# Queue positions of weight, joining and sample work, and ScalarE as issuer of attention stores, in a hybrid decoder step

## The chip, the cores and the metric

The kernel runs on one core of a Trainium2 chip. The core has a matrix engine (TensorE, PE in the rows; its weight loads are listed as PEld), a vector engine (VectorE, DVE), an activation engine (ScalarE, ACT), GpSimd (POOL) and SyncE (SP), which only issues transfers. Each engine takes its instructions in the order of its own queue, and an instruction that waits holds everything behind it. Transfers (DMAs) are issued from an engine's queue and then run on 16 DMA engines. The metric is the device time of one execution in microseconds (us); lower is better. Before and after are compared by the median of several executions; the trace comes from one further execution under the hardware profiler.

## What is computed

One layer of a hybrid decoder, for 2048 prompt positions and for 8 x 8 new tokens with a window buffer of 2048 positions. Cut to what matters:

```python
h = rms_norm(x, g_norm); proj = h @ w_in                 # u, va, za, q, k, vb, zb
vn = rms_norm(va per group); mixed = tril(w_s) @ vn + b_s # mixer A, chunks of 128
a = rms_norm(u * mixed) * silu(za)
for (w, r) in ((128, 1), (512, 4), (2048, 16)):          # mixer B, 8 heads x 64
    s = q @ k.T * SCALE, masked to w // r keys at stride r
    m = max(s); p = exp(s - m); den = sum(p)
    outs += p @ v / den; lses += m + log(den)
b = rms_norm(sum_i softmax(lses)_i * outs_i) * silu(zb)
h = x + concat(a, b) @ w_out
y = h + sigmoid(h @ w_ple_gate) * rms_norm(p_emb @ w_ple)
```

The new tokens take the same steps with the cached keys and values. Keys and values of the prompt and of the new tokens and the normalised `va` rows are outputs too.

## The kernel before, in words

**Phase 1, the projection.** `w_in` is cut into eight chunks, four of mixer A (384 columns) and four of mixer B (512 columns, one pair of heads), in the order A0 B0 B1 A1 B2 B3 A2 A3. For each chunk a loop runs over 16 tiles of 128 prompt rows and one tile of 64 new tokens. A tile is 24 matrix products (L473, `gemm`) into one of three PSUM banks (`psg`): values are held as a high and a low fp16 half, so three products stand for one. Then `a_evac` or `b_evac` empties the bank: copies, squares and a tanh on ScalarE (L613 to L616, L513 to L525), and as the last reader the gate product on VectorE (L617 or L526).

**Weights' steps.** While chunk n is multiplied, `wprep` prepares chunk n+1: loads (L351, SyncE), squares on ScalarE (L367), a sum over partitions by a matrix product with ones (L274), a chain of tiny VectorE steps for the scale, then the high half on ScalarE (L391) and the low half on VectorE (L392). `wprep3` does the same for `w_ple`, `w_out` and `w_ple_gate` (loads L940, squares L949, halves L964 and L965) during the last chunk and at the start of phase 2. The main loop calls one or more steps per tile with `next(nxt)`.

**Attention.** A planner (`Pump`) deals out attention in units between the projection's products. A unit is: scores on TensorE (L823), mask and maximum on VectorE (L829), exponential and high half on ScalarE (L838, L841), low half on VectorE (L842), a transposing DMA by SyncE (L763, `pT<-pc`), and the product with the values on TensorE (`stage_c`, L869 to L871, reading `pT`). After every second slot ScalarE copies the result out of PSUM (L875, `rec`) and SyncE stores it (L883, to `r1d`, `r2d` or `r3d` by stride). There are 160 units and 96 stores. Stride 16 is dealt in the last quarter of each head pair, ahead of four units of stride 4.

**Joining.** When a head pair has all three strides, `comb_load` loads them back (L891, `rl`) and `combine` weighs them, on VectorE for the most part (L901 to L926), and stores into `catd` (L928).

**Phase 2, per tile of 128 rows.** `p3_load` reads `catd` and x, `p3_cat` makes halves (L973 to L997) and transposes them by DMA (`Tc`), `p3_out` multiplies by `w_out`, `p3_h` does the same with the sum (`Th`), `p3_gate` multiplies by `w_ple_gate`, `p3_ple` by `w_ple` (all matrix products at L1008, `gemm2`).

**New tokens.** `sample` handles their attention for one head pair, cut into steps by `yield`: loads of cached keys and values, 16 multiplications on GpSimd (L1263) and 16 reductions on VectorE (L1264) per head pair, transposes and products on TensorE (L1243 to L1343). The planner deals these steps between phase 2's products.

**What sets the order.** The program is written in the order in which the planner deals, but a list scheduler then fixes each engine's queue: an instruction may stand ahead of one that was written earlier if, by the scheduler's own reckoning of time, its inputs are there first. `tc.issue_after(i)` adds a constraint of order only: what is written inside the block and goes to i's engine stands behind i in that engine's queue. Before, `behind()` uses it for `stage_c`, `a_mix` and some products of `sample`, always against the newest matrix product of the tile loop (`last_mm`).

## Time and profile before

| what | value |
|---|---|
| executions, us | 1469.55, 1474.05, 1478.37; median 1474.05 |
| profiled execution, us | 1471.11 |
| its span from first to last instruction, us | 1469.4 |
| mean granted TensorE clock | 0.954 |
| busy in the span: PE, DVE, ACT, POOL, us | 1296.9, 999.6, 821.8, 315.7 |
| chain of work that ended last, by kind | PE 44%, DMA 23%, DVE 14%, ACT 11% |

Times inside the trace count from the span's start. An engine counts as busy while an instruction of its own runs, not while it issues a transfer. A line of the timeline gives the start, the length, the engine, the source line and what was written from what; in square brackets stand the idle time of the engine just before it and what ended that. The list of waits adds such idle times up by who waited for whom.

### The profile page before, as it was taken

Reading aid. Unit: us, or ns where it says so; the run is one execution under the profiler, and the core shown is the slowest. Engines: PE = TensorE matmul, PEld = TensorE weight load, DVE = VectorE, ACT = ScalarE, POOL = GpSimd, SP = SyncE. Lnnn points to the kernel's source line nnn. Section 1 sums busy time; section 2 is a strip of 40 time slices with the busy share of each in tenths; the row PEclk is TensorE's granted clock in tenths of the full one; section 3 lists DMA queues with packets and bytes.
Section 4 is the critical chain, followed back from the end, with each engine's and each line's share of the span. In section 5 each row is a group of like instructions: output and inputs, shape, how many; then the busy total and the mean of one; then the engine's idle time right before and its main releaser. Section 6 shows DMA issues by size and latency. Waiting matters only on the chain.

```text
span 1469.4 us, 26262 instructions
## 1 busy us (share of the span) xinstructions
PE 1296.9 (88%) x8600; PEld 674.0 (46%) x8600; DVE 999.6 (68%) x3018; ACT 821.8 (56%) x2269; POOL 315.7 (21%) x279
## 2 busy tenths in 40 slices
PE   4899998998898897899788985569998998999998
PEld 2564454544564554455455653224443443444343
DVE  4675776777777698777778788885455456456364
ACT  5785778966679677687677884553222122123122
POOL 8221001102101111100120025311152143134001
PEclk9899999999999999999999998779999999999999
DMA  5954598799847989978996798976899799989542
GB/s 145 235 132 114 124 173 182 173 222 226 193 112 165 206 188 209 178 185 189 222 213 145 154 247 216 288 173 170 203 210 245 181 203 229 230 184 231 137 88 65
DMA packets 589592, 271.32 MB, mean 185 GB/s; under 512 B 323184, under 2 KB 571056, under 8 KB 589456
## 3 DMA queue, kind: packets, MB, share of 16 engines
q1 hardware_dynamic: 587472, 268.00, 80.7%
q0 software_dynamic: 1984, 1.66, 0.7%
q8 instruction: 67, 1.10, 0.3%
q14 instruction: 69, 0.57, 0.1%
HBM read 136.94 MB, written 55.08 MB: 131 GB/s over the span
## 4 chain that ended last, share of the span: by engine, by line
PE 44%; DMA 23%; DVE 14%; ACT 11%; issue 4%; SPq 3%; POOL 1%; DVEq 0%; ACTq 0%; POOLq 0%
PE psg L473 14%; PE psg L1008 11%; PE pss L1008 10%; DMA pT<-pc 6%; DMA rl<-r2d 2%; DVE sm L829 2%; ACT sm L838 2%; DMA K<-in_cache_k_dram 2%; DMA qB<-qd 2%; DMA wst<-in_w_in_dram 2%; PE pso L1343 2%; DVE pc L842 2%; PE pso L1248 2%; ACT kc L715 1%; DMA rl<-r3d 1%
## 5 line engine op out<-in xcount | busy, mean ns | idle before, releaser
L473 PE MATMUL psg<-wt,xT 128*128 128x512 f16 (+1 forms) x3072 | 640.6, 363 | 31.3 <-DVE agz L617 26.5
L473 PEld LDWEIGHTS <-xT 128*128 128x128 f16 x3072 | 301.7, 100 | 299.7 <-issue 44.3
L193 POOL TENSOR_TENSOR sm<-sm,mhalf 128x1 f32<-128x1 f32 (+5 forms) x115 | 145.6, 1271 | 790.4 <-DVE sm L532 324.6
L838 ACT ACTIVATE sm<-sm,rec 128x256 f32<-128x256 f32 (+1 forms) x384 | 151.7, 459 | 38.9 <-DVE rec L834 35.8
L829 DVE CUSTOM_DVE_ANT_0 sm<-pss,mask,psc 128x256 f32<-128x256 f32 (+1 forms) x384 | 145.1, 419 | 12.2 <-PE pss L823 8.5
L1008 PEld LDWEIGHTS <-Tc 128*128 128x128 f16 x800 | 76.8, 99 | 116.0 <-issue 28.5
L1263 POOL TENSOR_TENSOR K<-K,qB 96x512 f32<-96x512 f32 x64 | 94.1, 1475 | 161.2 <-DMA qB<-qd 62.3
L842 DVE TENSOR_TENSOR pc<-sm,pc 128x512 f16<-128x512 f32 (+1 forms) x160 | 104.2, 653 | 34.1 <-ACT pc L841 32.7
L1008 PEld LDWEIGHTS <-Th 128*128 128x128 f16 x800 | 76.7, 98 | 109.0 <-issue 15.3
L995 ACT ACTIVATE hl<-x,sm 128x1024 f16<-128x1024 f32 (+1 forms) x17 | 19.5, 1148 | 147.3 <-DVE sm L976 132.4
L869 PEld LDWEIGHTS <-pT 128*128 128x128 f16 x600 | 57.1, 98 | 96.1 <-DMA pT<-pc 90.5
L1008 PE MATMUL psg<-w,Th 128*128 128x512 f16 x400 | 95.8, 381 | 5.0 <-DMA Th<-hl 5.0
L841 ACT ACTIVATE pc<-sm 128x512 f16<-128x512 f32 (+1 forms) x160 | 96.0, 603 | 7.2 <-DMA pT<-pc 6.2
L1008 PE MATMUL psg<-w,Tc 128*128 128x512 f16 x400 | 97.0, 386 | 2.8 <-DMA Tc<-hl 2.8
L1264 DVE TENSOR_REDUCE blk<-K 96x8 f32<-96x512 f32 x64 | 43.4, 680 | 79.5 <-POOL K L1263 79.5
L1008 PE MATMUL pss<-w,Tc 128*128 128x512 f16 x400 | 96.0, 382 | 0.0
L1008 PE MATMUL pss<-w,Th 128*128 128x512 f16 x400 | 93.4, 379 | 0.0
L823 PEld LDWEIGHTS <-qk 128*128 128x128 f16 x960 | 74.2, 120 | 29.3 <-issue 5.9
L1100 POOL TENSOR_TENSOR tg<-tg,x 128x1024 f32<-128x1024 f32 (+1 forms) x16 | 37.6, 2348 | 153.9 <-DVE tg L1099 141.8
L869 PE MATMUL pso<-v,pT 128*128 128x65 f16 x248 | 32.2, 201 | 42.4 <-DMA pT<-pc 42.4
L869 PE MATMUL pso<-vt,pT 128*128 128x65 f16 x352 | 43.5, 195 | 28.9 <-DMA pT<-pc 28.8
L715 ACT ACTIVATE kc<-qk 128x512 f16<-128x512 f16 x72 | 58.9, 872 | 13.8 <-DMA qk<-qkd 8.5
(321 smaller groups left out, 2239.5 us busy)
## 6 DMA issues: line engine op xcount, KB each, us to landing
qB<-qd SPq DMA_DIRECT2D x64, 192.0 KB
K<-in_cache_k_dram SPq DMA_DIRECT2D x64, 192.0 KB
V<-in_cache_v_dram SPq DMA_DIRECT2D x64, 192.0 KB
vt<-vscr SPq DMA_DIRECT2D x32, 258.0 KB
K<-in_cache_k_dram SPq DMA_DIRECT2D x32, 256.0 KB
cat<-catd SPq DMA_DIRECT2D x16, 512.0 KB
x<-in_x_prompt_dram SPq DMA_DIRECT2D x16, 512.0 KB
V<-in_cache_v_dram SPq DMA_DIRECT2D x32, 256.0 KB
```

Of the source, the lines that this page charges most:

```text
L193: nc.gpsimd.tensor_tensor(y, src, mhalf[:p, :n], op=ALU.pow)
L473: last_mm[0] = nc.tensor.matmul(g[:, :ncol], lhsT=l, rhs=r, start=(n == 0), stop=(n == (23 if j < NT else 15)))
L715: nc.scalar.activation(t[:, h], src[:, h], AF.Copy)
L823: nc.tensor.matmul(pss[:, s, h, b * w:(b + 1) * w], lhsT=Q[:, h, qs], rhs=keys(h, k), start=(i == 0 and b == 0), stop=(i == 1 and b == n - 1))
L829: nc.vector.tensor_tensor_reduce(sm4[:, s, h], pss[:, s, h], mk, psc, -3.0e38, op0=ALU.add, op1=ALU.max, accum_out=mx[:, i:i + 1])
L838: nc.scalar.activation(sm4[:, s, h], sm4[:, s, h], AF.Exp, bias=r[:, sl + s, h, HD + 1:HD + 2])
L841: nc.scalar.activation(pc[:, :n], smv, AF.Copy)
L842: nc.vector.tensor_tensor(pc[:, n:2 * n], smv, pc[:, :n], op=ALU.subtract)
L869: nc.tensor.matmul(po[:, q, h, 0:65], lhsT=H, rhs=v[:, vs_, a:a + 65], start=(bi == 0), stop=False)
L1008: last_mm[0] = nc.tensor.matmul(gs[hf], lhsT=o[part][:, kt], rhs=w[:, kt % 2, half, :], start=(n[hf] == 0), stop=(n[hf] == (3 if m == P el ...
L1263: nc.gpsimd.tensor_tensor(K3, K3, qB, op=ALU.mult)
L1264: nc.vector.tensor_reduce(s3[:, b, :, ts_].rearrange("p h t -> p t h"), K3.rearrange("p t (h d) -> p t h d", d=HD), axis=AX.X, op=ALU.add)
```

## The change

Three things are changed.

1. `late()` is new. It puts what is written inside it behind the newest matrix product (`last_mm`), behind the newest full tile's gate on VectorE and tanh on ScalarE, and behind the newest transposing DMA on SyncE (of `pT`, or in phase 2 of a low half). In phase 2 the two marks of VectorE and ScalarE are renewed by `p3_out` and `p3_gate`. It wraps every step of `wprep` and `wprep3` that the tile loop or the planner calls, `combine`, and every step of `sample`. The first chunk's own weights and the steps left over at a chunk's end are not wrapped; neither are the loads of `comb_load`.
2. The 96 attention stores (L883 before, L898 after) and the 14 small copies of `fold` (L484 before, L494 after; the new tokens' half tiles) are issued by ScalarE instead of SyncE.
3. At the start, four of the eight loads of the first weights (L351) are issued by ScalarE.

```diff
+    last_on = {}
+
+    def late():
+
+        c = ExitStack()
+        for i in [last_mm[0]] + list(last_on.values()):
+            if i is not None:
+                c.enter_context(tc.issue_after(i.ins))
+        return c
...
-                    nc.sync.dma_start(t[:, k2, :ncol].rearrange("p (s c) -> p s c", c=P), src)
+                    (nc.scalar if fast and k2 else nc.sync).dma_start(
+                        t[:, k2, :ncol].rearrange("p (s c) -> p s c", c=P), src)
...
-        nc.sync.dma_start(c[:TS, :n], c[TS:, :n])
+        nc.scalar.dma_start(c[:TS, :n], c[TS:, :n])
...
+        tanh = nc.scalar.activation(th[:m], g[:m, 384:512], AF.Tanh, scale=sc[:m, 2:3])
+        gate = nc.vector.scalar_tensor_tensor(G["gz"][:m, q, :], th[:m], 1.0, g[:m, 384:512], op0=ALU.add, op1=ALU.mult)
+        if m == P:
+            last_on.update(dve=gate, act=tanh)
...
-                nc.sync.dma_start(o["pT"][:, :2 * o["n"] // P, :], o["pc"][:, :2 * o["n"]], transpose=True)
+                last_on["sp"] = nc.sync.dma_start(o["pT"][:, :2 * o["n"] // P, :], o["pc"][:, :2 * o["n"]], transpose=True)
...
-                combine(hp, jg, sc, *got)
+                with late():
+                    combine(hp, jg, sc, *got)
...
-            nc.sync.dma_start(dst[:, s0:s0 + 2], rc)
+            nc.scalar.dma_start(dst[:, s0:s0 + 2], rc)
...
-            yield from sample(hp)
+            steps = sample(hp)
+            while True:
+                with late():
+                    dt = next(steps, None)
+                if dt is None:
+                    break
+                yield dt
...
                 for _ in range(1 if ci else FIRST_PREP[j]):
-                    next(nxt, None)
+                    with late():
+                        next(nxt, None)
```

(`a_evac` is changed as `b_evac`; the two other calls of `next(nxt)`, in the last chunk and in phase 2, are wrapped likewise; the marks of `p3_out`, `p3_gate` and `halves_T` are single assignments.) All lines behind the new function stand 9 to 24 lines lower in the new file.

**Where it moves instructions.** First, one attention store, on SyncE before, in phase 1 (head pair 1; `pT<-pc` is a unit's transposing DMA, `rl` a load for joining):

```order
L763 DMA_TRANSPOSE pT_5315<-pc_5173 128x8x128
L891 DMA rl_6948<-r1d_108 128x4x132
L891 DMA rl_6950<-r2d_112 128x4x132
L686 DMA vt_5967<-vscr_100 128x1032
L883 DMA r2d_112<-rec_5013 128x264
L763 DMA_TRANSPOSE pT_5346<-pc_5198 128x8x128
L763 DMA_TRANSPOSE pT_5502<-pc_5333 128x8x128
```

The same store on ScalarE after:

```order
L626 ACTIVATE agz_5233,sm_5231<-psg_5499 128x128
L628 ACTIVATE th_5590<-psg_5499,sm_3646 128x128
L890 ACTIVATE rec_5013<-pso_5286 128x4x65
L898 DMA r2d_112<-rec_5013 128x264
L853 ACTIVATE sm_5322<-sm_5322,rec_5320 128x256 x2
L856 ACTIVATE pc_5333<-sm_5322 128x512
```

The store left its place ahead of two units' transposes on SyncE and now stands between ScalarE's own copy of the result and a unit's exponentials.

Second, VectorE near the end of the last chunk, before (L617 is the gate of the projection tile `psg_12784`, L965 makes a low half of `w_out`, L926 ends a joining, L669 ends a mixer A group, L1264 is a reduction for the new tokens):

```order
L965 SCALAR_TENSOR_TENSOR w_2247_12774<-w3st_12344,sm_12701,w_2247_12774 128x512
L926 TENSOR_TENSOR gzl_12559<-rl_12553,gzl_12559 128x512
L965 SCALAR_TENSOR_TENSOR w_2250_12809<-w3st_12346,sm_12701,w_2250_12809 128x512
L667 TENSOR_SCALAR sm_12755<-sm_12755,sm_10973 128x4
L965 SCALAR_TENSOR_TENSOR w_2250_12809<-w3st_12346,sm_12701,w_2250_12809 128x512
L965 SCALAR_TENSOR_TENSOR w_2251_12814<-w3st_12348,sm_12701,w_2251_12814 128x512 x2
L624 TENSOR_SCALAR sm_12824<-sm_12543,sm_10973 128x4
L617 SCALAR_TENSOR_TENSOR agz_12545<-th_12821,psg_12784 128x128
L965 SCALAR_TENSOR_TENSOR w_2269_12895<-w3st_12350,sm_12701,w_2269_12895 128x512 x2
L669 SCALAR_TENSOR_TENSOR ua_12195<-ua_12195,sm_12755,agz_12196 128x128 x4
L1264 TENSOR_REDUCE blk<-K_2453_13693 96x4x2
```

The gate of the same tile after (L629 there; L208 to L214 and L972 compute the scale of `w_ple`, L980 makes a low half of `w_ple`, L857 is a unit's low half):

```order
L681 TENSOR_SCALAR sm_12755<-sm_12755,sm_10973 128x4
L213 TENSOR_SCALAR sm_12165<-sm_12163 128x1
L214 TENSOR_SCALAR sm_12165<-sm_12163 128x1
L629 SCALAR_TENSOR_TENSOR agz_12545<-th_12821,psg_12784 128x128
L683 SCALAR_TENSOR_TENSOR ua_12195<-ua_12195,sm_12755,agz_12196 128x128 x2
L972 COPY sm_12168<-sm_12165 128x2
L683 SCALAR_TENSOR_TENSOR ua_12195<-ua_12195,sm_12755,agz_12196 128x128 x2
L642 TENSOR_TENSOR agz_12545<-agz_12545,gch_10877 128x512
L643 TENSOR_TENSOR ua_12544<-ua_12544,sm_12826 128x4x128
L1086 TENSOR_TENSOR sm_13247<-sm_12988,sm_12168 128x1
L857 TENSOR_TENSOR pc_12110<-sm_12091,pc_12110 128x512
L857 TENSOR_TENSOR pc_12249<-sm_12234,pc_12249 128x512
```

All of `w_out`'s low halves, and the reductions for the new tokens, now stand behind the gates of the last five projection tiles; before, 14 of those low halves stood ahead of this gate.

Third, TensorE at the end of attention, before (L871 reads the last unit's `pT`; L473 is the projection, L274 the sum over partitions for `w_out`):

```order
L871 LDWEIGHTS pT_12577
L871 MATMUL pso_12579<-vt_12230,pT_12577 128x65
L473 LDWEIGHTS xT_895
L473 MATMUL psg_12723<-wt_11147,xT_895 128x384
L274 MATMUL pso_12692<-sm_12612,ones 128x1
L473 LDWEIGHTS xT_895
L473 MATMUL psg_12723<-wt_11147,xT_895 128x384
```

The same place after (L886 for L871, L283 for L274, L1023 is phase 2's first product with `w_out`):

```order
L885 LDWEIGHTS pT_12577
L885 MATMUL pso_12579<-vt_12230,pT_12577 128x64
L886 LDWEIGHTS pT_12577
L886 MATMUL pso_12579<-vt_12230,pT_12577 128x65
L283 MATMUL pso_12692<-sm_12612,ones 128x1
L1023 LDWEIGHTS Tc_13122
L1023 MATMUL psg_13287<-w_2237_12703,Tc_13122 128x512
```

Attention's last unit and the sum for `w_out` moved from 153 projection products ahead of the projection's end to behind it; the fifth unit from the last (the last one of stride 16) moved from 246 to 60 products ahead of that end. Over all 160 units, the mean number of projection products between a unit's scores and its product with the values went from 63.5 to 69.3.

## Rows read from the trace of the kernel before

**Rows 1.** Busy time by stage: stretch, length, engines with instruction counts, clock, DMA, GB/s.

```profile
160.00:860.00 700.00, 622.82 (x5087) 361.90 (x5087) 535.14 (x1955) 525.26 (x1516) 98.94 (x69) 0.96 0.85 185
860.00:940.00 80.00, 49.25 (x303) 27.78 (x302) 65.56 (x149) 42.30 (x136) 32.03 (x27) 0.83 0.99 250
940.00:1000.00 60.00, 43.40 (x180) 18.31 (x179) 53.77 (x139) 35.51 (x87) 13.10 (x11) 0.83 0.85 205
1000.00:1350.00 350.00, 334.93 (x1667) 141.89 (x1666) 189.37 (x395) 81.93 (x188) 103.16 (x73) 0.98 0.92 209
1350.00:1470.00 120.00, 113.82 (x576) 49.19 (x573) 58.79 (x117) 29.41 (x63) 15.02 (x11) 0.99 0.46 106
```

**Rows 2.** TensorE's waits, whole span: who for whom, total us, times, longest us.

```profile
PE pso L869 <- DMA pT<-pc: 71.2, 57, 3.4
PE psg L473 <- DVE agz L617: 26.5, 3, 15.0
PE pst L1243 <- ACT KT L1253: 19.6, 6, 6.6
```

**Rows 3.** Timeline of four engines around the last projection tiles.

```profile
900.09 0.35 ACT L616 ACTIVATE th<-psg,sm 128x128 f32<-128x128 f32 x1
...
909.68 2.06 DVE L965 SCALAR_TENSOR_TENSOR w<-w3st,sm,w 128x512 f16<-128x512 f32 x3
...
911.80 0.27 DVE L617 SCALAR_TENSOR_TENSOR agz<-th,psg 128x128 f32<-128x128 f32 x1
...
912.13 5.70 PE L473 MATMUL psg<-wt,xT 128*128 128x384 f16 x24 [14.97 <-DVE agz L617]
...
927.76 0.38 ACT L613 ACTIVATE ua<-psg 128x256 f32<-128x256 f32 x1 [3.57 <-DMA catd<-ua]
...
929.03 0.80 PE L473 MATMUL psg<-wt,xT 128*128 128x384 f16 x2 [11.21 <-DVE agz L617]
```

**Rows 4.** Attention tiles' instructions: count, shortest/median/longest ns, first and last start.

```profile
L875 ACT ACTIVATE rec<-pso x96: 361/383/425, 161.7 to 880.8; 128x260 f32<-128x260 f32 x96
L883 SPq DMA_DIRECT2D r1d<-rec x32: 365/478/1178, 163.9 to 827.5; - x32
...
L763 SPq DMA_TRANSPOSE pT<-pc x160: 1188/1248/4225, 153.5 to 876.1; - x160
```

**Rows 5.** SyncE's waits for that copy, whole span.

```profile
SPq L883 <- ACT rec L875: 21.4, 21, 2.8
```

**Rows 6.** VectorE's waits for joining loads, ScalarE's for weight loads, whole span.

```profile
DVE sm L901 <- DMA rl<-r2d: 20.4, 10, 3.7
...
ACT junk L367 <- DMA wst<-in_w_in_dram: 31.4, 19, 4.6
```

**Rows 7.** The program's start: SyncE's issues, and ScalarE's last wait for weights.

```profile
1.93 6.45 SPq L351 DMA_DIRECT2D wst<-in_w_in_dram  x8
...
15.15 0.61 ACT L367 ACTIVATE junk<-wst,gno 128x384 bf16<-128x384 f32 x1 [1.06 <-DMA wst<-in_w_in_dram]
```

**Rows 8.** VectorE's low halves of chunk B0; TensorE's first B0 products.

```profile
96.90 4.71 DVE L392 SCALAR_TENSOR_TENSOR wt<-room,sm,wt 128x512 f16<-128x512 f32 x7
...
109.87 9.66 PE L473 MATMUL psg<-wt,xT 128*128 128x512 f16 x44
```

**Rows 9.** TensorE: end of the last stride-16 unit, then projection; phase 2's first `w_out` products.

```profile
857.27 0.20 PE L871 MATMUL pso<-vt,pT 128*128 128x65 f16 x1
857.30 10.07 PE L473 MATMUL psg<-wt,xT 128*128 128x384 f16 x61
...
939.18 2.75 PE L1008 MATMUL pss<-w,Tc 128*128 128x512 f16 x12
```

**Rows 10.** Pieces of the chain that ended last: start, us, what.

```profile
619.89 2.66 DMA r2d<-rec
...
891.91 5.07 DMA rl<-r2d
...
951.17 7.29 DMA Tc<-hl
```

**Rows 11.** Joining on VectorE: count, shortest/median/longest ns.

```profile
L910 DVE TENSOR_TENSOR rl<-rl,sm x48: 681/692/1762, 315.4 to 993.7; 128x520 f32<-128x520 f32 x48
L912 DVE TENSOR_TENSOR rl<-rl,rl x32: 682/689/694, 319.2 to 996.3; 128x520 f32<-128x520 f32 x32
```

**Rows 12.** New tokens' reductions on VectorE that ran between 860 and 939 us.

```profile
L1264 DVE TENSOR_REDUCE blk<-K x14: 670/674/685, 884.3 to 937.1; 96x8 f32<-96x512 f32 x14
```

More of the change, by code (lines that the diff above doesn't have):

```diff
@@ L524, in b_evac @@
         th = wk.tile([P, P], F32, name=nm("th"), tag="th", bufs=2)
-        nc.scalar.activation(th[:m], g[:m, 384:512], AF.Tanh, scale=sc[:m, 2:3])
-        nc.vector.scalar_tensor_tensor(G["gz"][:m, q, :], th[:m], 1.0, g[:m, 384:512], op0=ALU.add, op1=ALU.mult)
+        tanh = nc.scalar.activation(th[:m], g[:m, 384:512], AF.Tanh, scale=sc[:m, 2:3])
+        gate = nc.vector.scalar_tensor_tensor(G["gz"][:m, q, :], th[:m], 1.0, g[:m, 384:512], op0=ALU.add, op1=ALU.mult)
+        if m == P:
+            last_on.update(dve=gate, act=tanh)
     def b_norm(G, sc, gch):
@@ L615, in a_evac @@
         th = wk.tile([P, P], F32, name=nm("th"), tag="th", bufs=2)
-        nc.scalar.activation(th[:m], g[:m, 256:384], AF.Tanh, scale=sc[:m, 2:3])
-        nc.vector.scalar_tensor_tensor(G["gz"][:m, q, :], th[:m], 1.0, g[:m, 256:384], op0=ALU.add, op1=ALU.mult)
+        tanh = nc.scalar.activation(th[:m], g[:m, 256:384], AF.Tanh, scale=sc[:m, 2:3])
+        gate = nc.vector.scalar_tensor_tensor(G["gz"][:m, q, :], th[:m], 1.0, g[:m, 256:384], op0=ALU.add, op1=ALU.mult)
+        if m == P:
+            last_on.update(dve=gate, act=tanh)
     def a_norm(G, sc, gch):
@@ L997, in halves_T @@
         nc.vector.scalar_tensor_tensor(lo[:m], t[:m], r[:m], hi[:m], op0=ALU.mult, op1=ALU.subtract)
-        nc.sync.dma_start(dst[1], lo[:m], transpose=True)
+        last_on["sp"] = nc.sync.dma_start(dst[1], lo[:m], transpose=True)
         return o, mx, r
@@ L1054, in p3_out @@
             sl = slice(hf * 512, hf * 512 + 512)
-            nc.vector.scalar_tensor_tensor(h[:m, sl], gs[hf][:m], cm[:m], h[:m, sl], op0=ALU.mult, op1=ALU.add)
+            last_on["dve"] = nc.vector.scalar_tensor_tensor(h[:m, sl], gs[hf][:m], cm[:m], h[:m, sl], op0=ALU.mult, op1=ALU.add)
     def p3_h(j):
@@ L1095, in p3_gate @@
             sl = slice(hf * 512, hf * 512 + 512)
-            nc.scalar.activation(t[:m, sl], gs[hf][:m], AF.Tanh, scale=cm[:m])
+            last_on["act"] = nc.scalar.activation(t[:m, sl], gs[hf][:m], AF.Tanh, scale=cm[:m])
         dst = yp[j * P:(j + 1) * P] if j < NT else ysm
@@ L1474, in tile_hymba_gmlp_dilated_attn_step @@
                 for _ in range(1 if ci else FIRST_PREP[j]):
-                    next(nxt, None)
+                    with late():
+                        next(nxt, None)
             else:
                 for _ in range(LAST_PREP[j]):
-                    if next(nxt, None):
-                        break
+                    with late():
+                        if next(nxt, None):
+                            break
                 if j == 12:
@@ L1541, in tile_hymba_gmlp_dilated_attn_step, with deal @@
     last, cur, samp = None, 0, True
+    def deal():
+        with late():
+            next(nxt, None)
     for k in range(23):
-        pump.later(850.0 * (k + 1), lambda: next(nxt, None))
+        pump.later(850.0 * (k + 1), deal)
     p3_ple(0)
```

## The prediction

> **What bounds the kernel now.** I read the stages first. In the bulk of phase 1 TensorE is busy 622.8 of 700 us, with VectorE at 535.1 and ScalarE at 525.3 [rows 1]: TensorE leads, and the 77 us that it idles are the stake there. The list of waits says for what: 71.2 us over the whole span go to a unit's product with the values that waits for its transposing DMA, in 57 waits of at most 3.4 us (mean 1.25) [rows 2]. [...] From 1000 to 1350 TensorE is busy 334.9 of 350 [rows 1], so little can be had there beyond its own work.
>
> **Start.** SyncE issues the first eight weight loads one after the other in 6.45 us, and ScalarE's squares still wait 1.06 us for the last at 15.15 [rows 7]. With half of them on ScalarE the issue saves between 0 (if the transfer itself sets the end) and 3.2 us (half the issue). I take -1.5, near the middle, because the last wait left is small. Against that stands the second chunk's preparation: VectorE makes seven low halves in 4.71 us at 96.90, 8 us ahead of the first B0 product at 109.87 [rows 8]. In the new queue they stand behind the last full tile's gate, so this margin may go; between 0 and 3 us of it may show. I take +1.5. Together 0, between -3 and +3.
>
> **Stores moved to ScalarE.** SyncE loses 96 issues at a median of 478 ns, 46 us, and 21.4 us of waits for the copy that the store sends [rows 4, 5]; together 67 us over 160 units, 0.4 us per unit, by which its transposes can start earlier. ScalarE gets the 46 us: 525 + 46 = 571 of 700, 82%. That is still less than TensorE's 89%, and the 175 us that it idles hide it as long as an issue costs what it did on SyncE. ScalarE has issued no store of this kind in the trace of before, so the bounds are 0, when its idle time takes all (nothing lets a store on ScalarE save time on ScalarE, so no gain there), and 0.48 + 1.25 = 1.73 us per store, when each also waits for one SyncE transpose of 1248 ns [rows 4] or for the copy just ahead of it (383 ns, whose result must be written before it is sent). I take 0.48, hidden, since that row is the same operation with the same operands.
>
> **Waits for the transposed halves.** Over all units the distance between scores and product with the values grows by 69.3 - 63.5 = 5.8 projection products. A product is 10.07 / 61 = 0.165 us [rows 9] at 384 columns and 9.66 / 44 = 0.22 at 512 [rows 8], so a unit gets about 1.1 us more. If the 57 waits are spread evenly between 0 and 2.5, each falls by 0.86 on average, 49 us in all. The other bound is 0, since the order was worked out with a model of times and the products in between can themselves be held by VectorE or by the DMA engines (85% busy [rows 1]). I take -20, rather less than half: TensorE that runs ahead soon meets VectorE at 76%, and half the waits may turn into waits for gates.
>
> **Joining and start of phase 2.** Before, the last unit of stride 16 ends at 857.3, and the first `w_out` products come at 939.18 [rows 9]: 82 us, of which 26.2 are the two waits for gates [rows 3]. In the new order 186 more projection products stand ahead of that unit's end (246 - 60): 186 x 0.165 = 30.7 us. So it ends at 857.3 + 30.7 - 20 = 868. The projection has only 60 products, 10 us, left then, with no low half of `w_out` ahead of its gates; those waits vanish, and what is late next is a chain through the joining. From the pieces before: copy 0.4 and store issue 0.5 [rows 4], landing 2.7, load 5.1 [rows 10], joining on VectorE 3 x 0.69 + 2 x 0.69 [rows 11] and some 4 us of small steps and square roots (an estimate, as much again as the long ones), 16 low halves of `w_out` that now lie in the same stretch at 0.69 or 0.70, 11 us [rows 3], then store and load of `catd` (2.7 + 5.1) and the transposes of the halves, 7.3 [rows 10]. The sum is 42 us: 868 + 42 = 910, 29 us before 939. Bounds of the chain: 31, when VectorE makes `w_out`'s low halves while the chain waits for DMAs, and 50, when both landings and both loads take half as long again (8 us) at DMA engines that are 99% busy [rows 1]. VectorE gives a cross-check: its work in 860 to 1000 is 119 us [rows 1], less 9.4 for the 14 reductions that go behind [rows 12], 110 of 140; so this stretch cannot shrink by more than 30, and I use 9 of it (the other 20 come from phase 1).
>
> **Phase 2.** The reductions moved there are 14 x 0.674 = 9.4 us [rows 12] on a VectorE that idles 160 of 350 us [rows 1]: 0. The waits for joining loads on VectorE (20.4) and for weight loads on ScalarE (31.4) [rows 6] now hold less behind them, since what waits for a load stands behind a tile's gate and tanh and not ahead; that is how the -20 above can come about, not a further gain.
>
> **Sum.** 0 (start) + 0 (stores) - 20 (waits) - 9 (joining) + 0 (phase 2) = -29: 1471.1 - 29 = 1442 for an execution like the profiled one. The median of the runs is 2.9 above it, which gives **1445**.
>
> **Rivals.** *Slower: ScalarE becomes the bound.* If each store keeps ScalarE 1.73 us, 96 of them are 166 us and ScalarE stands at 691 of 700. Each added 1.25 us delays the exponentials and the copies that empty a bank; if a third of it reaches TensorE, that is 96 x 1.25 / 3 = 40 us, and the 20 of the waits are not won: -29 + 20 + 40 = +31, 1505. It decides from 0.6 us of wait per store (96 x 0.6 / 3 = 19, and half of the 20 lost, 10). For it speaks that SyncE's 32 issues into `r1d` took up to 1178 ns [rows 4], against it their median of 478. [...] *No difference.* The waits do not shrink, since the queues only follow a model's times, and the chain takes 50: 857.3 + 30.7 + 50 = 938, 1 us before 939: 1473. The coupling of all engines in [rows 1] speaks for it, the two waits for gates, which surely go, against it. *New tokens' loads come into phase 2.* The 14 reductions read 96 x 512 fp32 each, 197 KB; with as many values it is 5.5 MB, 26 us at 209 GB/s, in a stretch where the DMA engines are 92% busy and have 28 us left [rows 1]. If none fits, TensorE's waits for the new tokens' keys (19.6 us [rows 2]) more than double and it takes 1445 + 26 = 1471. Against it: the last 120 us have DMA engines at 46%. *Much faster.* All 49 us of the waits go: 1445 - 29 = 1416. That the change does not do what it says is ruled out by the order of the instructions, which shows the moves.
>
> **Chances.** Forecast 0.48 (1425 to 1462, from the waits' and the chain's bounds taken half way); much faster 0.13; no difference 0.12; new tokens' loads 0.08; slower 0.19. A measurement can tell about 0.5%, 1466.7 to 1481.4, from no change. Faster: 0.48 + 0.13 and a third of the two middle cases, which spread around 1472, less a little: 0.65. Same: the most of those, 0.14. Slower: 0.19 and the rest, 0.21. The range is 1411 to 1490: it leaves out the upper half of the slower case (0.1) and the lower end of the much faster one (some 0.06).
>
> **What would show it.** Right: no wait of TensorE for a gate above 3 us near the last projection tiles; waits for the transposes at about 50 us instead of 71; the last stride-16 unit's end near 868 and the first `w_out` product near 910; an issue of a store on ScalarE at about 0.5 us, and ScalarE busy or issuing about 570 us in 160 to 860. Wrong: issues on ScalarE of 1 us and more, with new waits of TensorE for exponentials or copies; a first `w_out` product after 930; new waits for the new tokens' keys above 40 us in phase 2; or a stall of some 3 us and more at the first B0 product.

## The result: 0.7% slower, with the projection's end 55 us earlier

The changed kernel takes 1483.93 us (median of 7 runs, 1481.43 to 1488.62) against 1474.05 for the kernel before: a ratio of 1.0066, 95% interval 1.0042 to 1.0090. The forecast was 1445 and faster. The measured time lies inside the range of 1411 to 1490, on the wrong side of no change. The profiled execution takes 1483.67 us with a span of 1481.9, so 12.5 more than the profiled one of before.

Busy time by stage of the kernel after, in the columns of [rows 1]:

```profile
160.00:860.00 700.00, 629.80 (x5176) 367.41 (x5174) 536.67 (x1958) 527.90 (x1543) 101.96 (x62) 0.99 0.86 182
860.00:940.00 80.00, 40.94 (x291) 22.75 (x289) 66.44 (x196) 56.88 (x161) 15.30 (x24) 0.77 0.84 235
940.00:1000.00 60.00, 49.59 (x211) 21.25 (x212) 47.44 (x102) 22.44 (x44) 18.57 (x12) 0.91 0.92 202
1000.00:1350.00 350.00, 331.56 (x1580) 135.38 (x1579) 182.59 (x375) 77.53 (x182) 97.84 (x76) 0.97 0.96 209
1350.00:1482.00 132.00, 119.61 (x580) 49.92 (x578) 67.52 (x138) 32.53 (x66) 21.04 (x15) 0.96 0.52 123
```

TensorE does 7 us more in 160 to 860 than in [rows 1], 8 less in 860 to 940 and 6 more in 940 to 1000. The stretch from the end of phase 1 to the first `w_out` products is called the passage from here on. TensorE's waits (who for whom, total us, times, longest):

```profile
PE pso L884 <- DMA pT<-pc: 61.3, 61, 3.5
PE psg L1023 <- DMA Tc<-hl: 33.7, 2, 31.4
...
PE pst L1285 <- DVE sm L989: 11.2, 2, 6.2
...
PE psg L1023 <- DMA Th<-hl: 9.8, 2, 5.4
PE pst L1258 <- ACT KT L1268: 7.5, 2, 6.1
```

The two waits for gates of [rows 2] are gone. In their place stands one wait of 31.4 us for the transposed halves of the first `cat` tile. TensorE's timeline shows where it falls (in brackets the idle time ahead of the instruction):

```profile
872.32 0.20 PE L886 MATMUL pso<-vt,pT 128*128 128x65 f16 x1
872.35 3.74 PE L483 MATMUL psg<-wt,xT 128*128 128x384 f16 x22
...
880.15 2.76 PE L483 MATMUL psg<-wt,xTs 128*128 128x384 f16 x16
...
924.01 1.03 PE L1023 MATMUL psg<-w,Tc 128*128 128x512 f16 x2 [31.43 <-DMA Tc<-hl]
```

The last unit of stride 16 ends at 872.5 (857.5 before) and the projection at 882.9 (938.0 before), 55 us earlier. The first `w_out` product comes at 924.0, 15.2 earlier than in [rows 9]. From there to TensorE's last product the same 2423 products (sample's, `w_out`, `w_ple_gate`, `w_ple`) take 551.8 us, where they took 524.6: 27.2 more. -15.2 + 27.2 = +12.0; the spans differ by 12.5, and the other half us lies behind TensorE's last product. So there are two questions: why 55 us became 15, and why phase 2 became 27 us longer.

A first answer to the second stands in TensorE's timeline where the new tokens' values are multiplied (L1343 before, L1358 after; `x8` is a group of four products of 32 columns each, since every product leaves two records, 128 for the 64 products). The kernel before:

```profile
1042.90 1.06 PE L1343 MATMUL pso<-V,blk 96*32 96x512 f32 x8
1043.89 1.47 PE L1008 MATMUL psg<-w,Tc 128*128 128x512 f16 x6
...
1049.18 1.06 PE L1343 MATMUL pso<-V,blk 96*32 96x512 f32 x8
1050.18 1.47 PE L1008 MATMUL psg<-w,Th 128*128 128x512 f16 x6
```

The kernel after:

```profile
1055.90 1.05 PE L1358 MATMUL pso<-V,blk 96*32 96x512 f32 x4
1056.88 0.82 PE L1023 MATMUL psg<-w,Tc 128*128 128x512 f16 x3
1057.63 1.04 PE L1358 MATMUL pso<-V,blk 96*32 96x512 f32 x2
1058.61 0.60 PE L1023 MATMUL pss<-w,Tc 128*128 128x512 f16 x2
1059.14 1.05 PE L1358 MATMUL pso<-V,blk 96*32 96x512 f32 x2
```

The step from one row to the next is what a row keeps TensorE for: 0.99 us for four products, 0.98 for two, 0.98 for one: one that stands alone costs as much as four that stand next to each other. An unbroken run of them in TensorE's queue is called a piece. The 16 groups stand in 26 pieces in the queue before and in 40 after. A piece took 0.98 to 1.00 us in all 26 before and in 38 of the 40 after; the other two, of two products each, took 1.79 us (at 1162.25) and 1.88 (at 1271.43). The step times of these products and of the small value products (L1339, the same in both) sum to 34.5 us before and 49.9 after: 15.4 of the 27. Of the rest, summed over all 2423 products, 5 us are longer waits (36.9 against 31.7). Products ran at the lower of the two granted clock levels that the traces show (0.50 and 1.00) for 30.2 us, against 23.4; as an fp16 product of 512 columns takes 0.43 us at the lower one and 0.22 at the upper one in both traces, about half of that time is loss, so this makes some 3 us of the difference. About 3 us remain without a name.

### The profile page after: what moved, and what is told of

Same layout as the page of the kernel before. It is cut to its first block, busy times and chain, and to the rows that moved or that the text cites. A ratio compares the mean times of both kernels' runs of the same rounds, so it can differ in the third digit from the quotient of the medians.

```text
span 1481.9 us, 26151 instructions
## 1 busy us (share of the span) xinstructions
PE 1301.5 (88%) x8600; PEld 669.4 (45%) x8600; DVE 993.2 (67%) x3018; ACT 820.9 (55%) x2269; POOL 308.0 (21%) x279
## 4 chain that ended last, share of the span: by engine, by line
PE 32%; DMA 25%; DVE 13%; ACT 13%; issue 6%; SPq 6%; POOL 3%; POOLq 0%; ACTq 0%; DVEq 0%
PE psg L483 14%; PE pss L1023 6%; DMA pT<-pc 5%; DMA K<-in_cache_k_dram 5%; PE psg L1023 5%; PE pso L1358 3%; ACT sm L853 2%; POOL K L1278 2%; ACT kc L729 2%; DVE sm L844 2%; DVE pc L857 1%; PE pss L838 1%; DMA qB<-qd 1%; DMA r3d<-rec 1%; SPq L777 1%
## 5 line engine op out<-in xcount | busy, mean ns | idle before, releaser
L483 PE MATMUL psg<-wt,xT 128*128 128x512 f16 (+1 forms) x3072 | 624.5, 357 | 8.8 <-DVE xT L453 2.9
L483 PEld LDWEIGHTS <-xT 128*128 128x128 f16 x3072 | 296.8, 99 | 270.5 <-issue 16.1
L1023 PEld LDWEIGHTS <-Tc 128*128 128x128 f16 x800 | 76.5, 98 | 142.3 <-DMA Tc<-hl 34.8
L1023 PEld LDWEIGHTS <-Th 128*128 128x128 f16 x800 | 78.8, 102 | 130.7 <-issue 40.2
L857 DVE TENSOR_TENSOR pc<-sm,pc 128x512 f16<-128x512 f32 (+1 forms) x160 | 103.7, 652 | 37.9 <-ACT pc L856 36.8
L1023 PE MATMUL psg<-w,Tc 128*128 128x512 f16 x400 | 96.7, 385 | 33.8 <-DMA Tc<-hl 33.7
L1278 POOL TENSOR_TENSOR K<-K,qB 96x512 f32<-96x512 f32 x64 | 83.9, 1314 | 134.2 <-DMA K<-in_cache_k_dram 87.6
L1023 PE MATMUL psg<-w,Th 128*128 128x512 f16 x400 | 102.9, 397 | 9.8 <-DMA Th<-hl 9.8
L1023 PE MATMUL pss<-w,Th 128*128 128x512 f16 x400 | 98.9, 392 | 0.2
L1023 PE MATMUL pss<-w,Tc 128*128 128x512 f16 x400 | 94.8, 379 | 0.0
L1268 ACT ACTIVATE KT<-pst 128x512 f32<-128x512 f32 x32 | 19.0, 594 | 91.7 <-PE pst L1258 91.6
L838 PE MATMUL pss<-kc,qk 128*128 128x128 f16 x704 | 60.8, 225 | 7.8 <-DVE sm L844 7.7
## 6 DMA issues: line engine op xcount, KB each, us to landing
cat<-catd SPq DMA_DIRECT2D x16, 512.0 KB
x<-in_x_prompt_dram SPq DMA_DIRECT2D x16, 512.0 KB
```

The costliest lines, as they stand in the source:

```text
L483: last_mm[0] = nc.tensor.matmul(g[:, :ncol], lhsT=l, rhs=r, start=(n == 0), stop=(n == (23 if j < NT else 15)))
L838: nc.tensor.matmul(pss[:, s, h, b * w:(b + 1) * w], lhsT=Q[:, h, qs], rhs=keys(h, k), start=(i == 0 and b == 0), stop=(i == 1 and b == n - 1))
L857: nc.vector.tensor_tensor(pc[:, n:2 * n], smv, pc[:, :n], op=ALU.subtract)
L1023: last_mm[0] = nc.tensor.matmul(gs[hf], lhsT=o[part][:, kt], rhs=w[:, kt % 2, half, :], start=(n[hf] == 0), stop=(n[hf] == (3 if m == P el ...
L1278: nc.gpsimd.tensor_tensor(K3, K3, qB, op=ALU.mult)
```

## The experiments

All times are medians. The chips differ by up to 11 us for the kernel before, so a kernel is compared with the kernel before on its own chip (the ratio). e1 to e4, e5 to e8, e9 to e12 and e13 to e16 ran on one chip each. "First w_out" is the start of phase 2's first `w_out` product, "phase 2" the time from there to TensorE's last product, both from the profiled execution. These columns come from one execution each and carry its noise: e8 and e16 are the same kernel on two chips and give 920.2 and 937.5, 522.0 and 529.5. So between chips a difference of up to 17 us in the start, or 8 us in phase 2, is no evidence alone, and the 15 us by which the changed kernel's first `w_out` product came earlier lean on the ratios of e13 to e15 below.

| run | us | before there | ratio (95% interval) | projection ends | first w_out | phase 2 |
|---|---|---|---|---|---|---|
| before (profiled) | 1474.05 | | | 938.0 | 939.2 | 524.6 |
| after | 1483.93 | 1474.05 | 1.0066 (1.0042 to 1.0090) | 882.9 | 924.0 | 551.8 |
| e1 | 1469.19 | 1475.94 | 0.9968 (0.9940 to 0.9996) | 886.9 | 940.0 | 523.5 |
| e2 | 1479.85 | 1475.94 | 1.0013 (0.9989 to 1.0037) | 917.2 | 922.8 | 550.0 |
| e3 | 1489.79 | 1475.94 | 1.0090 (1.0061 to 1.0119) | 912.7 | 916.7 | 562.1 |
| e4 | 1474.59 | 1475.94 | 1.0000 (0.9973 to 1.0028) | 924.3 | 954.2 | 512.0 |
| e5 | 1458.56 | 1473.10 | 0.9917 (0.9890 to 0.9944) | 879.1 | 922.1 | 528.6 |
| e6 | 1463.06 | 1473.10 | 0.9922 (0.9892 to 0.9952) | 880.2 | 928.3 | 527.5 |
| e7 | 1464.42 | 1473.10 | 0.9950 (0.9925 to 0.9976) | 885.3 | 926.7 | 529.7 |
| e8 | 1452.76 | 1473.10 | 0.9878 (0.9846 to 0.9909) | 878.2 | 920.2 | 522.0 |
| e9 | 1480.45 | 1483.78 | 0.9968 (0.9942 to 0.9994) | 954.1 | 955.2 | 522.3 |
| e10 | 1468.02 | 1483.78 | 0.9875 (0.9810 to 0.9941) | 890.7 | 923.9 | 534.2 |
| e11 | 1468.07 | 1483.78 | 0.9878 (0.9825 to 0.9932) | 915.8 | 919.9 | 538.9 |
| e12 | 1468.07 | 1483.78 | 0.9874 (0.9820 to 0.9928) | 888.5 | 931.3 | 531.3 |
| e13 | 1464.59 | 1481.70 | 0.9881 (0.9834 to 0.9927) | 922.8 | 928.4 | 535.2 |
| e14 | 1466.19 | 1481.70 | 0.9885 (0.9828 to 0.9941) | 923.0 | 929.0 | 531.3 |
| e15 | 1480.73 | 1481.70 | 0.9987 (0.9965 to 1.0009) | 937.0 | 938.1 | 536.8 |
| e16 | 1466.10 | 1481.70 | 0.9895 (0.9844 to 0.9947) | 895.7 | 937.5 | 529.5 |

### Which part costs, and which gains: e1 to e4

e1 takes `late()` from the new tokens' steps alone:

```diff
-                with late():
-                    dt = next(steps, None)
+                dt = next(steps, None)
```

> The changed kernel, but the new tokens' steps are not put behind anything (no late() around sample); all else as changed. In the changed kernel phase 2 takes 551.8 us from the first w_out product (924.0) to TensorE's end against 524.6 before, and in its program the groups of four value products for the new tokens (L1358) stand in 40 pieces, before in 26; here they stand in 26 again. Theory A (queue positions of the new tokens' steps cost phase 2 its time): phase 2 takes 527 +-6, the projection still ends near 883, the first w_out product comes at 920 to 930, time about 1457. Rival B (phase 2 is longer because phase 1's earlier end leaves it the same work in a stretch whose DMA engines are full): phase 2 stays at 545 to 555, time 1478 to 1486.

Phase 2 is back at 523.5, as theory A said. But the first `w_out` product did not stay at 920 to 930: it came at 940.0, as before, although the projection had ended at 886.9. TensorE's waits in e1 between 870 and 965:

```profile
PE psg L1023 <- DMA Tc<-hl: 42.4, 2, 41.6
```

So most of the lead of 51 us at the projection's end turned into a wait of 41.6 us for the first `cat` tile. That was not expected, nor was the time of 1469.19 (about 1457 was); it means that the other parts of the change, without late steps of the new tokens, gain nothing at the start of phase 2.

e2 is the opposite: the kernel before, with `late()` around the steps of `sample` and nothing else.

> The kernel before with one part of the change alone: the steps of sample are put behind the tile ahead; stores and loads on SyncE as before, weights' steps and joining as before. Its groups of value products stand in 37 pieces (before 26). Theory A: phase 1 as before (projection ends at 935 to 940), first w_out product at 930 to 940, phase 2 543 to 552 instead of 524.6, time 1485 to 1495. Rival B: phase 2 as before, time 1462 to 1472.

Phase 2 takes 550.0 us, so theory A holds there. Its miss is the passage: the projection ends at 917.2 and the first `w_out` product comes at 922.8, 16 us earlier than before, from this part alone. Passage and phase 2 nearly cancel in the time (1.0013).

e3 is the changed kernel with the stores, fold copies and first loads on SyncE; e4 is the kernel before with stores and fold copies on ScalarE:

```diff
-            nc.scalar.dma_start(dst[:, s0:s0 + 2], rc)
+            nc.sync.dma_start(dst[:, s0:s0 + 2], rc)
```

> The changed kernel with all its queue positions, but the attention stores, fold copies and first weight loads issued by SyncE as before. Theory C (queue positions alone make the 55 us by which the projection ends earlier, 882.9 against 938.0): projection ends at 880 to 895, time within 8 us of the changed kernel, 1476 to 1492. Rival D (the stores on ScalarE free SyncE, and the transposes' earlier issue makes most of it): projection ends after 910, time 1500 and more. Rival E (the stores on ScalarE cost TensorE time): projection ends before 875.

> The kernel before with ScalarE issuing the 96 attention stores and the 14 fold copies, nothing else. Its value products for the new tokens stand in 33 pieces (before 26), which by theory A costs 7 us. Theory C: projection ends at 928 to 938 (SyncE relieved by 0.4 us per unit), time 1472 to 1481. Rival D: projection ends before 910, time under 1460. Rival E: projection ends after 940, time over 1485.

Both stand between the theories. Without the stores on ScalarE the projection ends 30 us later (912.7), which theory C did not allow, but the first `w_out` product comes no later (916.7), and the time, by the ratios (1.0090 against 1.0066, with intervals that overlap), is some 4 us longer, not 17 and more. The stores alone make the projection end 14 us earlier and change nothing in the time (1.0000): the first `w_out` product comes 15 us later than before, at 954.2, and phase 2 takes 12.6 us less. e4 also warns against reading phase 2's length as the price of pieces alone. Its 33 pieces do cost what theory A says (the value products' steps sum to 42.4 us, 7.9 more than before), but TensorE's waits in phase 2 fall from 31.7 to 14.0. So an earlier end of the projection by itself is worth nothing in e4, and in e1 little (its ratio lies 0.3% under 1).

### Is the splitting the cost? e5 to e8

e5 is the changed kernel; only the order within a group of value products is bound. The product of the values that are loaded last goes first, and the other three stand behind it:

```diff
-                with behind():
-                    for b, v in zip(quad, V3):
+                lead = None
+                for b, v in reversed(list(zip(quad, V3))):
...
-                        nc.tensor.matmul(acc[q0:q0 + 32], lhsT=wz[:96, q0:q0 + 32], ...)
+                    with behind() if lead is None else tc.issue_after(lead.ins):
+                        mm = nc.tensor.matmul(acc[q0:q0 + 32], lhsT=wz[:96, q0:q0 + 32], ...)
+                    lead = lead or mm
```

> The changed kernel, but in each group of four value products for the new tokens (L1358) the product of the last loaded values is written first and the other three are put behind it in TensorE's queue, so that the 16 groups stand in 16 pieces (changed kernel: 40; before: 26). Each piece of one to four products takes about 1 us on TensorE. Theory A1 (the splitting is the larger part of phase 2's loss of 27 us): start-to-start time of the value products falls from 49.9 to about 26 us, phase 2 from 551.8 to about 530, time 1458 to 1470. Rival F (the group now waits for the last of its four loads, and TensorE idles instead): waits of TensorE for values of 15 us and more, phase 2 stays over 545, time 1477 and more.

Theory A1 holds. By the ratios (0.9917 against 1.0066) the time is 22 us under the changed kernel's, and phase 2 takes 528.6, 23 less. The timeline shows whole groups again, and the price of rival F, the wait for the last of four loads:

```profile
1055.40 1.06 PE L1359 MATMUL pso<-V,blk 96*32 96x512 f32 x8
1056.40 1.04 PE L1023 MATMUL pss<-w,Tc 128*128 128x512 f16 x4
1057.27 0.38 PE L1023 MATMUL psg<-w,Th 128*128 128x512 f16 x1
1058.32 1.06 PE L1359 MATMUL pso<-V,blk 96*32 96x512 f32 x8 [0.67 <-DMA V<-in_cache_v_dram]
1059.32 1.90 PE L1023 MATMUL psg<-w,Th 128*128 128x512 f16 x8
1061.75 1.06 PE L1359 MATMUL pso<-V,blk 96*32 96x512 f32 x8 [0.54 <-DMA V<-in_cache_v_dram]
```

Over all groups that price is 6.2 us in 6 waits (idle time ahead of the products of L1359 and of their weight loads; ahead of the products alone it is 2.3 us in 3):

```profile
  DMA V<-in_cache_v_dram: 6.2, 6
```

The value products' steps fall from 49.9 to 24.8 us. TensorE's waits in phase 2 do not fall (41 us in all, 36.9 in the changed kernel), and neither does the time of products at the lower clock level (31.1 us, 30.2 there), so that part of its loss is not mended by this.

A mark is the instruction that `late()` puts others behind; from e6 on `late()` can be given the engines whose marks it uses beside TensorE's. e6 removes only SyncE's mark from the new tokens' steps, e7 leaves them late for the first head pair alone, e8 adds the bound groups to e7:

```diff
-                with late():
+                with late(('dve', 'act')):                          # e6
+                with late() if hp == 0 else nullcontext():          # e7, e8
                     dt = next(steps, None)
```

> The changed kernel, but the new tokens' steps are not put behind the newest transposing DMA on SyncE (they still are behind the marks on TensorE, VectorE and ScalarE). The value products then stand in 24 pieces. Theory G (it is SyncE's mark that delays the loads and so splits the groups and makes the waits): phase 2 520 to 532, first w_out product at 920 to 930, time 1450 to 1462. Rival H (the marks on VectorE and ScalarE make the waits): the split goes, waits and half clock stay, phase 2 536 to 545, time 1466 to 1474.

> The changed kernel, but only the new tokens' steps of the first head pair, whose reductions fall in the passage from phase 1 to phase 2, are put behind the tile ahead; those of the other three are free as before. 32 pieces of value products. Theory A2 (late steps help in the passage, where VectorE joins, and hurt after it): first w_out product at 922 to 927, phase 2 530 to 537, time 1457 to 1468. Rival B: phase 2 stays at 545 and more, time 1475 and more.

> As e7_first_pair_late, and with the value products in groups of four as in e5_glued (16 pieces). Theory A2 with A1: 16 fewer pieces at about 1 us each, phase 2 515 to 525, time 1440 to 1455. Rival F: as e7_first_pair_late or slower.

e6 (phase 2 at 527.5, first `w_out` product at 928.3) says that in the changed kernel SyncE's mark splits the groups: with it the loads of values stand behind the newest transposing DMA, without it the queue has 24 pieces again. The likely reason, not tested by itself, is that the scheduler deals the four products out one by one as it reckons that each load lands; in e4, which uses no `late()`, they stand in 33 pieces, so marks are not the only thing that splits. On the chip this protects from little, as the 6.2 us of e5 show. e7 came as expected, within half a us. e8, with late steps in the passage only and with whole groups, is the fastest of these four: 1452.76, ratio 0.9878. It beats the kernel before and the changed one.

### What each other part is worth: e9 to e12

e9 is the kernel before with bound groups:

> The kernel before, with one thing changed: the 16 groups of four value products for the new tokens stand in 16 pieces instead of 26. In the three kernels measured so far a piece costs 1.0 us whatever its one to four products (before: 25.7 us in 26; changed: 41.0 in 40; glued: 15.9 in 16). Theory A1 (the piece is the unit of cost, independent of the rest of the change): phase 2 from the first w_out product falls from 524.6 by 10 to 515 +-4, time 1460 to 1468. Rival F2 (before, TensorE has slack there, or the groups then wait for values): phase 2 stays within 3 us of 524.6, time 1470 to 1478.

The piece costs the same here (the value products' steps fall from 34.5 to 24.8 us), but the ratio is 0.9968, some 5 us and not 10. TensorE's waits in phase 2 sum to 38.6 us where the kernel before has 31.7, so part of the gain goes into waits; the comparison is across chips, so how much is not settled. Phase 2, at 522.3, stayed where rival F2 put it; neither theory's times held.

e10, e11 and e12 each take one part out of e8: `late()` around the steps of `w_ple`, `w_out` and `w_ple_gate`; the stores and fold copies on ScalarE; and `late()` around the weights' steps of the first chunk:

```diff
-                    with late():
-                        if next(nxt, None):
-                            break
+                    if next(nxt, None):                             # e10
+                        break
...
-            nc.scalar.dma_start(dst[:, s0:s0 + 2], rc)
+            nc.sync.dma_start(dst[:, s0:s0 + 2], rc)                # e11
...
-                    with late():
+                    with late() if ci else nullcontext():           # e12
                         next(nxt, None)
```

> e8_first_pair_late_glued (1452.8; projection ends at 878.2, first w_out product at 920.2), but the steps of w_ple, w_out and w_ple_gate are not put behind the tile ahead. Theory J (what stands between the projection's end and the first w_out product is the chain through the joining; the weights' steps only fill it): the projection ends later, at 890 to 905, since gates wait again for low halves of w_out, but the first w_out product stays at 917 to 925, time 1449 to 1458. Rival K (the late weights' steps hold up the joining on VectorE and ScalarE): first w_out product before 913, time under 1446. Rival L: the gate waits come back in full (26 us) and the first w_out product goes to 930 and more, time over 1460.

> e8_first_pair_late_glued with the attention stores and fold copies issued by SyncE again. In the changed kernel's queues the stores on ScalarE made the projection end 30 us earlier (912.7 without, 882.9 with), the time only 6 us shorter. Theory J (the joining's chain, and not the projection, sets the first w_out product): projection ends at 905 to 915, first w_out product at 914 to 922, time 1449 to 1459. Rival M (the stores' gain comes through once phase 2 is mended): time 1465 and more.

> e8_first_pair_late_glued, but during the first chunk the weights' steps are not put behind the tile ahead. The first product of the second chunk came at 111.6 before and at 115.7 in the changed kernel (113.2 in e8). Theory N (the low halves behind the last gate cost 2 to 4 us at that border, and this reaches the end): first product of the second chunk at 110 to 112, time 1448 to 1452. Rival: the 2 us are lost again before phase 2, time 1451 to 1456.

All three give the ratio that e8 had on its chip: 0.9875, 0.9878 and 0.9874 against 0.9878. With four executions each the intervals reach 0.6% to either side, so a part worth less than that would not show. Theory J's places held nearly (projection at 890.7 and 915.8, first `w_out` product at 923.9 and 919.9); the absolute times that were expected did not, since this chip takes longer for the kernel before too (1483.78). e11 and e12 side by side say most: with the stores on ScalarE the projection ends 27 us earlier (888.5 against 915.8), and the time is the same, 1468.07 in both. In e12 TensorE waits 33.2 us for the first `cat` tile, in e11 4.6:

```profile
PE psg L1023 <- DMA Tc<-hl: 34.9, 2, 33.2
```

```profile
PE psg L1023 <- DMA Tc<-hl: 4.6, 1, 4.6
```

What theory N asked, whether 2 us at the first border reach the end, stays open: the interval is wider than that. (The times that its expectation names for that border are not those of the traces, where the first product of the second chunk starts at 109.87 before, 111.18 in the changed kernel, 109.88 in e8 and 113.26 in e12.)

### What makes the passage's gain: e13 to e16

e13 is the kernel before with two edits, `late()` for the first head pair's new-token steps and bound groups. e14 and e15 are e13 with fewer marks, and e16 is e8 again on the same chip (the lines stand against those of the changed kernel):

```diff
+                with late() if hp == 0 else nullcontext():                   # e13
+                with late(("sp",)) if hp == 0 else nullcontext():            # e14
+                with late(("dve", "act")) if hp == 0 else nullcontext():     # e15
                     dt = next(steps, None)
```

> The kernel before with two edits: the new tokens' steps of the first head pair are put behind the tile ahead, and the value products stand in 16 pieces. Weights' steps, joining and stores as before. Theory P (the passage's gain comes from the first pair's reductions and loads leaving it, nothing else): first w_out product 14 to 18 us earlier than in the kernel before, phase 2 520 to 530, ratio to the kernel before 0.985 to 0.991, the same as e16. Rival Q (the weights' steps, joining and stores carry part of it): ratio 0.993 to 0.998, e16 at 0.988.

> As e13_first_pair_alone, but behind the marks on TensorE and SyncE only (the latter holds the loads of cached keys back; the reductions follow their data). Theory R (the loads' traffic and place on SyncE decide): as e13_first_pair_alone within 0.4%. Rival S (VectorE's and ScalarE's queues decide): first w_out product at most 6 us earlier than before, ratio 0.993 and more.

> As e13_first_pair_alone, but behind the marks on TensorE, VectorE and ScalarE only, so that the loads are issued as early as before. Theory R: first w_out product at most 8 us earlier than before, ratio 0.992 and more. Rival S: as e13_first_pair_alone within 0.4%.

> The kernel of e8_first_pair_late_glued (first pair late, glued groups, and all other parts of the change) on this chip, as what e13 is compared with: ratio to the kernel before 0.985 to 0.991. Theory P: the same as e13 within 0.4%. Rival Q: 0.5% or more below e13.

Theory P holds in the ratio: e13 gives 0.9881, e16 0.9895. Weights' steps, joining and stores, most of the change, carry nothing that can be measured with four executions each and intervals of half a per cent to either side. Its numbers for the trace did not hold (phase 2 at 535.2, not 520 to 530; first `w_out` product 11 us earlier than before, not 14 to 18), and e16's first `w_out` product came 9 us later than e13's in the profiled executions without a longer median; the profiled execution of e16 is the slowest of its four (1474.86). Theory R holds too: SyncE's mark alone does as much (0.9885), the marks on VectorE and ScalarE without it nothing (0.9987). e13 and e15, which differ in that mark alone, lie 16 us apart in time, on one chip. So what the passage gains is that the first pair's loads, of cached keys (`K`) and of copies of the queries (`qB`), leave it. SyncE's issues in e1, where they are free, between the load of the last stride-16 results and the store of the first joined tile:

```profile
890.45 0.54 SPq L906 DMA_DIRECT2D rl<-r3d  x1
...
902.90 2.17 SPq L1274 DMA_DIRECT2D K<-in_cache_k_dram  x1
905.16 0.47 SPq L906 DMA_DIRECT2D rl<-r2d  x1
910.00 0.48 SPq L1274 DMA_DIRECT2D K<-in_cache_k_dram  x1
910.69 3.81 SPq L1277 DMA_DIRECT2D qB<-qd  x3
914.59 3.59 SPq L1274 DMA_DIRECT2D K<-in_cache_k_dram  x2
918.28 1.11 SPq L943 DMA_DIRECT2D catd<-gzl  x1
```

and in the changed kernel, where none lies between:

```profile
885.95 0.53 SPq L906 DMA_DIRECT2D rl<-r3d  x1
...
896.65 0.36 SPq L906 DMA_DIRECT2D rl<-r2d  x1
...
905.60 0.37 SPq L943 DMA_DIRECT2D catd<-gzl  x1
906.01 0.51 SPq L906 DMA_DIRECT2D rl<-r3d  x1
```

27.8 us against 19.7. The other traces agree. Counted in the same stretch, SyncE issues none of these loads in the twelve kernels where it takes 18.0 to 21.5 us, 10 in e15 and 11 in e6 (24.8 in both), 18 in e1, and 23 to 27 in the kernel before, e9 and e4 (33.5 to 43.2), where VectorE makes the pair's reductions there as well. e6 keeps theory R from being the whole account: without SyncE's mark, but with the reductions behind the gates and all other parts of the change, only 11 loads stayed in the stretch, and the first `w_out` product came at 928.3, near the 920 to 927 of e5, e7 and e8 on the same chip, and not at 940 as in e1. In the kernel before those two marks do nothing, in the changed one they do much of it.

In e13 and e14 the gain reaches the first `w_out` product by another way than in the changed kernel: the projection's end comes earlier (922.8 and 923.0, against 937.0 in e15), with less waiting for gates. TensorE's waits in e13, then in e15:

```profile
PE psg L483 <- DVE agz L629: 5.2, 1, 5.2
```

```profile
PE psg L483 <- DVE agz L629: 13.9, 2, 7.2
```

Why gates wait longer beside the loads was not tested. Whether the loads hold the joining by their place in SyncE's queue or by their traffic (DMA engines 96% busy in 860 to 940 in e1, 84% in the changed kernel) was not told apart.

## Why the prediction was wrong, point by point

- **Start: within its bounds.** The four loads on ScalarE won nothing: ScalarE's squares of the last load came at 15.26 (15.15 before). The low halves behind the gate cost what was feared. TensorE waited 0.80 and 1.41 us at the first B0 products, which came at 111.18 (109.87 before):

```profile
111.18 0.59 PE L483 MATMUL psg<-wt,xT 128*128 128x512 f16 x2 [0.80 <-ACT wt L401]
113.18 5.01 PE L483 MATMUL psg<-wt,xT 128*128 128x512 f16 x15 [1.41 <-DVE wt L402]
```

- **Stores: hidden, as put; the slower rival did not come.** An issue on ScalarE took less than the 478 ns of [rows 4], not 1.73 us; the 96 issues took 35.0 us in all, and 50.2 on SyncE before (count, shortest/median/longest ns):

```profile
L898 ACTq DMA_DIRECT2D r1d<-rec x32: 372/377/437, 166.4 to 836.1; - x32
L898 ACTq DMA_DIRECT2D r2d<-rec x32: 326/338/412, 181.9 to 892.6; - x32
L898 ACTq DMA_DIRECT2D r3d<-rec x32: 326/327/1145, 283.7 to 877.3; - x32
```

The bound of 1.73 us, in which every store also waits out a transpose of SyncE, was an estimate from [rows 4], and ScalarE's issues do not show it: of the 96 the longest took 1145 ns, beside an issue of 1519 ns on SyncE that ended 15 ns after it, and the 64 into `r1d` and `r2d` stayed under 440. SyncE's side leaves room for a small cost: its 160 transposes took 234.7 us to issue, 223.5 before, and over all traces 229.7 to 239.1 with the stores on ScalarE, 222.3 to 229.5 without. That is some 0.05 us for one, and no run shows that it costs time.

- **Waits for transposed halves and gates: the place right.** The former fell by 10 us (71.2 to 61.3), half of the 20, and the gates' 26 us went as said. With 10 in place of 20 the forecast's sum puts the end of the last stride-16 unit at 878; it came at 872.5, where 868 was forecast, and what made up the difference was not taken apart. The projection ended at 882.9, where 878 follows from the forecast.

- **The joining's chain: right in kind, too short by 10 us.** 42 us were summed, 51.5 measured (872.5 to 924.0). Two parts were mis-sized. ScalarE copied the unit's result only 4.3 us after its products, behind squares for `w_out` and exponentials, and from the store's issue to the load's issue passed 8.7 us, where 0.5 + 2.7 had been set. The load stood in SyncE's queue behind three transposes of other units, which kept it until 885.86; the sum had no term for that queue:

```profile
876.85 0.38 ACT L890 ACTIVATE rec<-pso 128x260 f32<-128x260 f32 x1
877.25 0.33 ACTq L898 DMA_DIRECT2D r3d<-rec  x1
```

```profile
872.95 12.91 SPq L777 DMA_TRANSPOSE pT<-pc  x3
885.95 0.53 SPq L906 DMA_DIRECT2D rl<-r3d  x1
```

The rest nearly cancels: from that load to the store of the joined tile 19.7 us where 23.6 were summed, from there to the first `w_out` product 18.4 where 15.1 were.

So the first `w_out` product came 15 us earlier, not 29. The forecast also gave this gain to the wrong part: e1, e2 and e13 to e15 show that it hangs on the first pair's loads, which the sum did not price, and e1 that without it the time won in phase 1 is lost in the wait for `cat`. Nor could more than a few of the gates' 26 us be won while the joining stayed as it was: before, the transposition of the first `cat` tile's high half was issued at 931.0, only 7 us ahead of the projection's end:

```profile
931.04 2.99 SPq L996 DMA_TRANSPOSE Tc<-hl  x1
```

- **Phase 2: the step that failed.** The sum said 0, from the reductions on VectorE alone, 9.4 us beside 160 idle. It measured +27. `late()` also moved the new tokens' products on TensorE, the engine that bounds phase 2 (busy 334.9 of 350 us in [rows 1]), and their loads. The value products lost their groups (15 us; e5 gets 25 us of their steps back by binding them), with 5 us of waits and some 3 at the lower clock level beside it. e1 confirms the term as a whole: without late steps of the new tokens phase 2 takes 523.5 us. The rival that brought the new tokens into phase 2 looked at the right place and at the wrong mechanism: TensorE's waits for their keys fell, from 19.6 to 7.5 us. The order of the queue, which was at hand, showed the groups in 40 pieces. What the order cannot show is that one product costs as much as four; the timeline of the kernel before shows that too, where a product stands alone (0.98 us to the next row):

```profile
1158.18 1.04 PE L1343 MATMUL pso<-V,blk 96*32 96x512 f32 x2
1159.16 0.39 PE L1008 MATMUL psg<-w,Th 128*128 128x512 f16 x1
```

The sum with measured terms: -15 for the passage, +27 for phase 2 and the half us at the end give +12.5, and 1471.1 + 12.5 = 1483.6.

## What to carry to other kernels

Instructions that cost together what each costs alone, as the four value products here (0.99 us against 0.98), are one piece of work: before steps are re-queued, count the pieces that such groups stand in, and bind them if a scheduler may take them apart. A stage that ends earlier gains only what its successor's inputs allow (15 of 55 us here): find the chain that feeds the next stage, here stores, loads, joining and transposes, before time is taken off the stage. Of a step that is moved, price its instructions on the engine that bounds the place where they go, not only on the engine where they hurt before.

## What the hardware showed

Four fp32 products with 32 columns of weights each, standing next to each other on TensorE, took 0.99 us together, two took 0.98 and one alone 0.98. The time that four neighbours save against four products that stand alone goes when other products stand between them: in the traces of before and after, 26 and 40 pieces summed to 25.7 and 41.0 us. The issue of a store into `r1d` took 377 ns in the median on ScalarE, where the same stores took 478 on SyncE [rows 4].
